# Two-layer backbone (window attention, latent attention): other homes and load points for norm weights, raw group weights, latent rows and rotary buffers; block sums of the first token half in three steps

## The chip, the core and the metric

The kernel runs on one core of one Trainium2 chip. A core has five engines that each work through their own instructions in order and meet at semaphores: TensorE (PE, matmuls and transposes; PEld its weight loads), VectorE (DVE), ScalarE (ACT), GpSimd (POOL) and SyncE (SP), which here mainly issues DMA transfers. The metric is the device time of one execution in microseconds, from runs on the chip; less is better.

## The reference

One batch of 1024 latent tokens and 256 context tokens, 1024 features, two layers. Layer 0 is grouped-query attention in a window (16 query heads, 4 key heads), layer 1 is multi-head latent attention; each layer is `x += gate * mixer(adaLN(rms_norm(x)))`. The change lies in the projections of layer 1:

```python
def project(h):                                   # h: 1024 latent + 256 context rows
    cq, ckv, kr, g = jnp.split(h @ w_in, [512, 768, 800], axis=-1)
    q = (rms_norm(cq, q_norm) @ w_uq).reshape(b, n, 16, 64 + 32)
    kv = (rms_norm(ckv, kv_norm) @ w_ukv).reshape(b, n, 16, 64 + 64)
    return q[..., :64], q[..., 64:], kv[..., :64], kr, kv[..., 64:], g

qrx = apply_rope(qrx, cos, sin); krx = apply_rope(krx, cos, sin)
s = (einsum("bqhd,bkhd->bhqk", qn, kn) + einsum("bqhd,bkd->bhqk", qr, kr)) * scale
y = (softmax(s) @ v * silu(g)) @ w_out
```

Everything is float32.

## The kernel before

**Arithmetic.** A float32 product is made of three PE products: each factor is split into a high part, rounded to the fast matmul format (a cast on ACT, L125), and the rest (a subtraction on DVE or POOL, L126); `mm3` then multiplies high by high, low by high and high by low (L130, L131, L132). So most operands pass ACT and then DVE or POOL before PE may use them.

**Memory.** On-chip memory is laid out by hand. Arena `F` has 52 slots of 1 KB per partition for float32 work, the arenas `R` and `K` hold split operands. A `Ring` is a list of places in an arena that are handed out in turn, over and over. Whatever is written into a place waits until its former content has been read; so the choice of places is also a choice of waits. Matmul results go to eight PSUM banks (`PB`).

**Order.** Up to the attention of layer 1 the order of instructions on each engine is set by a scheduler from the order in which the program is written, the dependences and its own estimates of durations; only the attention of layer 1 is ordered by hand. SP issues most DMAs, in order; small loads (`load2`) are issued by ACT.

**The stage that the change touches** is the projection of layer 1, L986 to L1400, from about 700 to 960 us of the span:

- `norm_x` (L229 to L234) loads 128 rows of x, takes the mean square (ACT L231), the power (POOL L233) and scales (DVE L234). `turn_h` transposes two such tiles on PE (L245), applies scale and shift on ACT into an x slot of 8 KB (L249; ring `xtr`), and splits (L253, L254).
- `kv_tile` multiplies one tile of 128 tokens with 288 columns of b_w_in, 24 products into one of three banks. The first 256 columns are the latent keys: normed with `rstd` (L1025 to L1027) and the weight `kvn` (DVE L1065); the other 32 are the rotary key (copied by ACT, L1066, which lets go of the bank). Then they are turned (L1071), split and written to `ckv_d` (L1075). The weight `kvn` is loaded on ACT's queue (L1042) into F 13, where the last output projection of layer 0 still adds its result (L706).
- `t_sums` builds, from two x slots, the sums of token blocks that the fast matrix product needs (Strassen-Winograd, seven products of half size in place of eight): T1 to T4, each split by a cast (L1100) and a subtraction (L1101). The sums L1095 to L1097 and L1104 are made in place, in the x slots.
- `Group` is one such product, 256 columns of b_w_in by all tokens. Groups 0 and 1 give the query latents (`cq`), groups 2 to 5 the gate. `fetch` loads raw weights (L1119) into the ring `wr`, `op` makes their sums on DVE (L1138 to L1152) in the ring `sr` and splits them (POOL makes the low part), `P(n)` does the products, adds earlier ones on DVE (L1172, L1178, L1186) into the ring `ov`, and `post` sends the result to DRAM: L1194 to `g_d` after a silu (L1193), L1200 to `cq_d`.
- `kr_rope` (L1085 to L1089) applies the rotary embedding to all keys, with two buffers of ring `er`, which shares F 8 to 10.5 with `sr`.
- `load_rows`, `scale_rows` bring the query latents back, norm and split them; `qr_tile` multiplies them with the rotary part of b_w_uq (block 3, `fetch1(3)`), `rope` (L281, L286, POOL L291) writes into the ring `ev` with temporaries from `rtmp`, and the result is turned (L1251) and written to `qr_d` from the ring `qst`. `qn_tile` does the other part. All weights of this part pass the staging ring `stg`.

Of the kernel before, what the change touches and what calls it, by code (L numbers as in the profile page):

```python
# [31 lines left out]
B_SCALE = 96 ** -0.5  # L32
# [28 lines left out]
def kernel(ctx: ExitStack, tc: tile.TileContext, t, out, dbg=None):  # L61
# [926 lines left out]
    sinb = f_at(1, 8, 32)  # L988
    kvn = f_at(13, 256)
    er = Ring(F, [8 + 1.25 * i for i in range(4)], 320)  # L990
# [4 lines left out]
    t4buf = f_at(4, 4, 256)  # L995
    p1s = [f_at(o, 512) for o in (22, 24, 49, 2, 49, 2)]
    ov = Ring(F, [34, 45, 47, 4, 6], 512)
    sr = Ring(F, [8, 10, 12], 512)
    sqacc = [f_at(37, 512), f_at(39, 512)]
    r_b = [f_at(41, 512), f_at(43, 512)]  # L1000
    cqr = Ring(F, [14, 16, 18, 20, 30, 32, 26, 28], 512)
    stg = Ring(F, [30, 32.25, 49.5], 576)
# [29 lines left out]
    for p in range(2):  # L1032
        xs = [norm_x(src1(2 * p + j), xr, junk) for j in range(2)]
        xts[p] = shp(xtr.next(), 8, 256)
        turn_h(p, xs, xts[p], hT1[p], ada1, range(4))
    load2(out=cosb, in_=t["cos_b"].rearrange("p (t d) -> p t d", t=8))
    load2(out=sinb, in_=t["sin_b"].rearrange("p (t d) -> p t d", t=8))
    for _ in last_outproj:
        pass
    load2(out=qncol, in_=t["q_norm_col"])  # L1040
    nc.vector.tensor_scalar_mul(qncol, qncol, B_SCALE)
    load2(out=kvn, in_=t["b_kv_norm"].partition_broadcast(128))  # L1042

# [38 lines left out]
    def kr_rope():  # L1082
        u = krF[:, 2:10, :]
        o, tmp = [shp(er.bufs[i], 8, 32) for i in range(2)]
        nc.vector.tensor_mul(o, u, cosb)  # L1085
# [5 lines left out]
    def t_sums(x0, x1, cs, t4):  # L1091
# [10 lines left out]

        put(T2, hb)
        sub(t4, lb, hb)  # L1104
        put(T1, la)
        put(T3, ha)
        return lambda: put(T4, t4)

# [99 lines left out]
    def latent_rms(step):  # L1208
# [15 lines left out]
        nc.gpsimd.tensor_tensor(rc, rc, mhalf.to_broadcast([128, 8]), ALU.pow)  # L1224

    def load_rows(h):
        rows = [cqr.next() for c in range(4)]
        for c, u in enumerate(rows):
            load(out=u, in_=cq_d[c, :, 512 * h : 512 * h + 512])
        return rows  # L1230
# [57 lines left out]
    def first_op(i, n):  # L1288
        groups[i].fetch((n - 1,), 1)
        groups[i].op(n)  # L1290

    t_rest = []
    order1 = [2 * p + j for p in (0, 1, 3, 2, 4) for j in range(2)]
    nx = norm_x(src1(order1[4]), xr, junk)
    for i, ti in enumerate(order1):
# [22 lines left out]
        if i == 3:  # L1318
            t_rest.append(t_sums(xts[1], xts[3], slice(0, 256), t4buf))
        if i in (5, 7):  # L1320
# [4 lines left out]
        if i > 7:  # L1325
            first_op(0, i - 7)
            first_op(1, i - 7)
        if i == 8:
            groups[0].P(1)
    groups[1].P(1)  # L1330
    flush()
    t_rest.append(t_sums(xts[2], xts[4], slice(256, 512), xts[2][:, 4:8]))
    wr = Ring(F, [30, 26], 1024)
    for f in t_rest:
        f()
    groups[0].fetch()
    groups[0].P(2)
# [3 lines left out]
    groups[1].fetch()  # L1341
    kr_rope()
    for gi, ns in todo:
        g = groups[gi]
        last = gi == 5
        ops = [] if last else list(todo[gi + 1][1])
        for i, n in enumerate(ns):
# [6 lines left out]
            if gi == 4 and i in (1, 3):  # L1354
                latent_rms(i)
            if gi == 4 and i == 5:
                rows = [load_rows(0)]
            if last and i == 0:
                rows.append(load_rows(1))
            if last and i == 2:  # L1360
                stg = Ring(F, [8, 10, 12, 22, 24], 512)
                fetch1(3)
            if last and i in (4, 5):
                scale_rows(i - 4, rows[i - 4])
    fetch1(4, nc.vector)
    ev = Ring(F, [34, 45, 47, 6], 512)
    rtmp = Ring(F, [49, 2], 512)
    qst = Ring(F, [14, 18, 30, 37, 41, 26], 1024)
    for ti in range(8):
# [550 lines left out]
```

## Time and profile before

| | |
|---|---|
| median of 3 runs | 1581.6 us (1580.81 to 1582.58) |
| the profiled execution | 1577.52 us, its span 1575.7 us |
| PE, DVE, ACT, POOL busy | 97%, 66%, 51%, 51% of the span |
| mean granted clock of PE | 0.988 |
| instructions | 25723, of them 9190 matmuls and transposes |

The span runs from the first to the last instruction of the profiled execution; its own time is 1.8 us longer. A row of the timeline reads: start and busy time in us, engine, line of the kernel, operation, what it writes, what it reads, shape, and in brackets how long the engine idled just before and what ended the idle time. A row of waits reads: engine, target and line, what ended the wait, then us in total, times, and the longest in us. A row of windows reads: the stretch in us, its length, busy time (and instructions) of PE, PEld, DVE, ACT and POOL, PE's granted clock as a share of full speed, the share of the DMA engines, GB/s. The names `arena_f`, `arena_r` and `arena_k` stand for any place in an arena.

### The profile page before, as it was taken

What the parts mean: (1) busy time and instruction counts of PE and PEld (TensorE: products, weight loads), DVE (VectorE), ACT (ScalarE), POOL (GpSimd) and SP (SyncE); (2) the same over time, 40 slices, a digit from 0 to 9 for tenths busy, and PEclk for the clock granted to TensorE, in tenths of its full rate; (3) what the DMA queues carried; (4) which work ended last, traced back from release to release, by engine and by line L of the source; (5) the groups of instructions that cost most, each with busy time, mean ns of one, the idle gap of its engine ahead of it and who ended that gap; (6) DMA issues with size and microseconds to landing.
All of it is one profiled execution on the core that took longest, in us unless ns stands there. A gap on an engine that the chain in (4) does not pass through costs nothing. (4 is left out here: it accounts for less than half of the span.)

```text
span 1575.7 us, 25723 instructions
## 1 busy us (share of the span) xinstructions
PE 1523.3 (97%) x9190; PEld 1187.6 (75%) x9190; DVE 1045.0 (66%) x1745; ACT 803.0 (51%) x1550; POOL 804.5 (51%) x840
## 2 busy tenths in 40 slices
PE   7999999999999999997989999999999999999998
PEld 4988888887878888877868778666766766766687
DVE  3878996657777777766654543677577677577354
ACT  4432322267777777767733523555555555555321
POOL 1151211136565444543375542688688688689410
PEclk9999999999999999998999999999999999999999
DMA  8357674653343333334354576223233232243251
GB/s 324 102 163 218 199 207 136 199 163 100 100 145 99 87 94 89 91 113 148 111 158 132 175 260 190 85 70 98 62 96 100 73 94 84 62 137 113 69 167 67
DMA packets 160078, 204.01 MB, mean 129 GB/s; under 512 B 14656, under 2 KB 94016, under 8 KB 159952
## 3 DMA queue, kind: packets, MB, share of 16 engines
q1 hardware_dynamic: 158480, 200.48, 42.5%
q10 hardware_dynamic: 1472, 1.90, 0.4%
q8 instruction: 72, 1.18, 0.3%
q14 instruction: 54, 0.44, 0.1%
HBM read 151.46 MB, written 50.87 MB: 128 GB/s over the span
## 5 line engine op out<-in xcount | busy, mean ns | idle before, releaser
L130 PE MATMUL PB<-arena_r 128*128 128x512 f32 (+2 forms) x990 | 368.8, 375 | 11.9 <-ACT arena_r L125 6.8
L1565 POOL TENSOR_TENSOR arena_f<-arena_f 128x512 f32<-128x512 f32 x252 | 328.4, 1303 | 82.0 <-ACT arena_f L1557 65.2
L131 PE MATMUL PB<-arena_r 128*128 128x512 f32 (+2 forms) x958 | 352.7, 369 | 1.3 <-POOL arena_r L685 0.8
L132 PE MATMUL PB<-arena_r 128*128 128x512 f32 (+2 forms) x926 | 339.7, 367 | 0.0
L126 POOL TENSOR_TENSOR arena_r<-arena_f,arena_r 128x512 fp32r<-128x512 f32 x106 | 148.1, 1409 | 280.9 <-ACT arena_r L125 231.0
L130 PEld LDWEIGHTS PB<-arena_r 128*128 128x128 f32 x990 | 187.5, 190 | 47.7 <-ACT arena_r L125 7.9
L1557 ACT ACTIVATE arena_f<-PB 128x1024 f32<-128x1024 f32 x160 | 164.1, 1026 | 109.4 <-PE PB L1551 69.1
L1516 DVE TENSOR_REDUCE arena_f<-PB 128x1 f32<-128x1024 f32 x128 | 156.0, 1218 | 86.4 <-PE PB L1514 86.3
L131 PEld LDWEIGHTS PB<-arena_r 128*128 128x128 f32 x958 | 182.4, 190 | 29.7 <-DVE arena_r L420 2.4
L132 PEld LDWEIGHTS PB<-arena_r 128*128 128x128 f32 x926 | 176.7, 191 | 29.0 <-issue 1.7
L1551 PE MATMUL PB<-arena_r 64*128 64x512 f32 (+1 forms) x1490 | 194.4, 392 | 0.3 <-ACT arena_f L1557 0.3
L1551 PEld LDWEIGHTS PB<-arena_r 64*128 64x128 f32 (+1 forms) x1490 | 135.8, 185 | 29.0 <-ACT arena_f L1557 1.8
L126 DVE TENSOR_TENSOR arena_r<-PB,arena_r 128x512 fp32r<-128x512 f32 (+1 forms) x171 | 115.7, 684 | 60.5 <-ACT arena_r L125 59.6
L1573 PE MATMUL PB<-arena_f 128*64 128x512 f32 x640 | 144.4, 597 | 0.0
L628 DVE CUSTOM_DVE_ANT_0 arena_f<-PB,arena_f,small 128x640 f32<-128x640 f32 (+2 forms) x176 | 125.1, 722 | 18.5 <-PE PB L617 11.8
L631 ACT ACTIVATE arena_f<-arena_f,small 128x640 f32<-128x640 f32 (+2 forms) x160 | 119.5, 747 | 34.8 <-DVE small L628 32.1
L125 ACT CAST arena_r<-arena_f 128x512 fp32r<-128x512 f32 (+1 forms) x139 | 83.5, 617 | 93.5 <-PE PB L132 26.4
L125 ACT CAST arena_r<-PB 128x512 fp32r<-128x512 f32 (+1 forms) x171 | 98.2, 582 | 46.0 <-PE PB L648 44.0
L617 PE MATMUL PB<-arena_k,arena_r 128*128 128x256 f32 (+1 forms) x576 | 111.6, 309 | 1.5 <-DVE small L628 1.3
L1573 PEld LDWEIGHTS PB<-arena_f 128*64 128x64 f32 x640 | 43.1, 136 | 83.2 <-issue 79.7
L648 PE MATMUL PB<-ident,arena_f 128*128 128x128 f32 x672 | 103.9, 274 | 0.8 <-DVE arena_r L126 0.3
L617 PEld LDWEIGHTS PB<-arena_k,arena_r 128*128 128x128 f32 x576 | 89.5, 188 | 14.1 <-DVE small L628 3.5
(246 smaller groups left out, 2634.2 us busy)
## 6 DMA issues: line engine op xcount, KB each, us to landing
arena_f<-ada_w SPq DMA_DIRECT2D x40, 512.0 KB, 4.7
arena_r<-q_d SPq DMA_DIRECT2D x80, 256.0 KB, 3.8
arena_r<-qn_d SPq DMA_DIRECT2D x64, 256.0 KB, 4.0
arena_r<-qr_d SPq DMA_DIRECT2D x170, 64.0 KB, 3.3
arena_f<-a_w_in SPq DMA_DIRECT2D x40, 256.0 KB, 3.5
g_d<-arena_f SPq DMA_DIRECT2D x32, 256.0 KB
q_d<-arena_f SPq DMA_DIRECT2D x64, 128.0 KB, 2.5
qn_d<-arena_f SPq DMA_DIRECT2D x16, 512.0 KB, 3.0
```

The source lines that it names most:

```text
L125: nc.scalar.copy(hi, src)
L126: (lo_eng or nc.vector).tensor_sub(lo, src, hi.bitcast(F32))
L130: nc.tensor.matmul(o, ah, bh, start=first, stop=False, skip_group_check=more)
L131: nc.tensor.matmul(o, al, bh, start=False, stop=False, skip_group_check=more)
L132: nc.tensor.matmul(o, ah, bl, start=False, stop=last, skip_group_check=more)
L617: nc.tensor.matmul(S[:, at : at + n], qT[:, s, hq, :], kT[:, g, k : k + n], start=s == 0, stop=s == 1)
L628: nc.vector.tensor_tensor_reduce(P[:, a:b], S[:, 256 + a : 256 + b], mk, 1.0, sk, ALU.add, ALU.min, to)
L1516: nc.vector.reduce_max(mx[:, 32 + b : 33 + b], flat, AX.X, negate=True)
L1551: nc.tensor.matmul(S[:, t], k[r, c : c + 128], q[r], start=j == 0, stop=j == 4)
L1557: nc.scalar.activation(E, self.S, AF.Exp)
L1565: eng.tensor_add(self.acc, self.acc, E[:, t])
L1573: nc.tensor.matmul(self.pv[p : p + 64], Vq[:, cs[t], self.h % 4, :], E[:, t], start=i == 0, stop=i == 4)
```

## The change

The change gives several buffers other places in arena F and moves some loads and a few computations in the written order. It adds no computation and takes none away.

- `kvn` lies in F 51 and is loaded ahead of the last output projection of layer 0, as is `qncol`.
- `t_sums` is a generator with three steps: the fourth sum and T1, then T2 and T3, then T4. For the first token half the first step follows the fourth kv tile, the second the sixth; for the second half both come at the end. T4 comes last for both.
- Group weights: the ring `wr` of the large pieces lies in F 22 and 26 in place of 30 and 26, and group 0's large pieces are fetched in the loop, at the last kv tile. First products (`p1s`), outputs (`ov`) and sums (`sr`, five places up to group 3, then three) have other places.
- `kr_rope` uses the place of `junk` (F 34.5) and runs ahead of the second products of groups 0 and 1.
- The first half of the latent rows is asked for in group 3, the second at the end of group 4, in F 22 and 24 in place of 30 and 32. The weights of the rotary part are loaded by the new `load_qr` in group 4, in a ring of three places, and split in group 5. That ring of three also stages all later weights, in place of five. `ev`, `rtmp` and `qst` have other places.

```diff
@@ -986,19 +986,19 @@
-    kvn = f_at(13, 256)
+    kvn = f_at(51, 256)
...
-    p1s = [f_at(o, 512) for o in (22, 24, 49, 2, 49, 2)]
-    ov = Ring(F, [34, 45, 47, 4, 6], 512)
-    sr = Ring(F, [8, 10, 12], 512)
+    p1s = [f_at(o, 512) for o in (45, 47, 49, 2, 45, 47)]
+    ov = Ring(F, [34, 30, 32, 4, 6], 512)
+    sr = Ring(F, [8, 10, 12, 41, 43], 512)
...
-    cqr = Ring(F, [14, 16, 18, 20, 30, 32, 26, 28], 512)
+    cqr = Ring(F, [14, 16, 18, 20, 22, 24, 26, 28], 512)
@@ -1033,13 +1033,13 @@
+    load2(out=qncol, in_=t["q_norm_col"])
+    nc.vector.tensor_scalar_mul(qncol, qncol, B_SCALE)
+    load2(out=kvn, in_=t["b_kv_norm"].partition_broadcast(128))
     load2(out=cosb, in_=t["cos_b"].rearrange("p (t d) -> p t d", t=8))
     load2(out=sinb, in_=t["sin_b"].rearrange("p (t d) -> p t d", t=8))
     for _ in last_outproj:
         pass
-    load2(out=qncol, in_=t["q_norm_col"])
-    nc.vector.tensor_scalar_mul(qncol, qncol, B_SCALE)
-    load2(out=kvn, in_=t["b_kv_norm"].partition_broadcast(128))
@@ -1081,7 +1081,7 @@
     def kr_rope():
         u = krF[:, 2:10, :]
-        o, tmp = [shp(er.bufs[i], 8, 32) for i in range(2)]
+        o, tmp = [f_at(34.5 + i, 8, 32) for i in range(2)]
@@ -1100,11 +1100,13 @@
-        put(T2, hb)
         sub(t4, lb, hb)
         put(T1, la)
+        yield
+        put(T2, hb)
         put(T3, ha)
-        return lambda: put(T4, t4)
+        yield
+        put(T4, t4)
@@ -1223,6 +1225,14 @@
+    def load_qr(ks):
+        sts = []
+        for k in ks:
+            st = stg.next()
+            load(out=st, in_=t["b_w_uq"][k * 128 : k * 128 + 128, 1024:1536])
+            sts.append(st)
+        return sts
@@ -1316,7 +1325,10 @@
         if i == 3:
-            t_rest.append(t_sums(xts[1], xts[3], slice(0, 256), t4buf))
+            t13 = t_sums(xts[1], xts[3], slice(0, 256), t4buf)
+            next(t13)
+        if i == 5:
+            next(t13)
@@ -1325,24 +1337,29 @@
+        if i == 9:
+            wr = Ring(F, [22, 26], 1024)
+            groups[0].fetch()
         if i == 8:
             groups[0].P(1)
     groups[1].P(1)
     flush()
-    t_rest.append(t_sums(xts[2], xts[4], slice(256, 512), xts[2][:, 4:8]))
-    wr = Ring(F, [30, 26], 1024)
-    for f in t_rest:
-        f()
-    groups[0].fetch()
+    t24 = t_sums(xts[2], xts[4], slice(256, 512), xts[2][:, 4:8])
+    next(t24)
+    next(t24)
+    kr_rope()
+    for f in (t13, t24):
+        next(f, None)
     groups[0].P(2)
     groups[1].P(2)
     for n in todo[0][1]:
         groups[0].op(n)
     groups[1].fetch()
-    kr_rope()
     for gi, ns in todo:
         g = groups[gi]
         last = gi == 5
+        if gi == 4:
+            sr = Ring(F, [8, 10, 12], 512)
@@ -1353,19 +1370,24 @@
-            if gi == 4 and i == 5:
+            if gi == 3 and i == 1:
                 rows = [load_rows(0)]
-            if last and i == 0:
+            if gi == 4 and i == 6:
                 rows.append(load_rows(1))
+                stg = Ring(F, [8, 10, 12], 512)
+                qrw = load_qr((0, 1, 2))
             if last and i == 2:
-                stg = Ring(F, [8, 10, 12, 22, 24], 512)
-                fetch1(3)
+                wt1[3] = r_at(wst1[3], 2, 4, 512)
+                for k in range(4):
+                    split(wt1[3][:, 0, k], wt1[3][:, 1, k], qrw[k], nc.gpsimd)
+                    if k == 0:
+                        qrw += load_qr((3,))
...
-    ev = Ring(F, [34, 45, 47, 6], 512)
-    rtmp = Ring(F, [49, 2], 512)
-    qst = Ring(F, [14, 18, 30, 37, 41, 26], 1024)
+    ev = Ring(F, [49, 2, 37, 39], 512)
+    rtmp = Ring(F, [41, 43], 512)
+    qst = Ring(F, [14, 18, 22, 26, 30, 45], 1024)
```

What the scheduler makes of it is shown at three places, as it stands in the engines' queues (line, operation, target, sources, shape; in the changed kernel the lines behind L1100 are two or more higher).

The first place is ACT around the third kv tile. The piece of the difference shows where the load of `kvn` stood.

```order
 L249 ACTIVATE arena_f<-PB,small 128x256
-L1042 DMA arena_f<-b_kv_norm 128x256
-L253 CAST arena_r<-arena_f 128x512
 L1025 ACTIVATE arena_f,small<-PB 128x256
-L125 CAST arena_r<-arena_f 128x512
+L253 CAST arena_r<-arena_f 128x512
 L1025 ACTIVATE arena_f,small<-PB 128x256
 L125 CAST arena_r<-arena_f 128x512
 L1066 COPY krF<-PB 128x32
 L231 ACTIVATE arena_f,small<-arena_f 128x1024
+L125 CAST arena_r<-arena_f 128x512
```

The load is gone from here; it now stands in the middle of layer 0's attention, some 240 rows earlier on ACT. The transposes of the next x tiles (L245) also stand elsewhere on PE: behind 7 products of the fourth kv tile, where there were 15.

The second place is DVE at the block sums of the first token half: L1104 (L1103 in the changed kernel) is the fourth sum, L1101 the low parts, of T2 in `arena_k`, of T1 and T3 in `arena_r`.

```order
 L234 TENSOR_SCALAR arena_f<-arena_f,small 128x1024
-L1104 TENSOR_TENSOR arena_f<-arena_f 128x1024
-L1101 TENSOR_TENSOR arena_k<-arena_f,arena_k 128x4x256
-L1101 TENSOR_TENSOR arena_r<-arena_f,arena_r 128x4x256 x2
+L1103 TENSOR_TENSOR arena_f<-arena_f 128x1024
+L1101 TENSOR_TENSOR arena_r<-arena_f,arena_r 128x4x256
 L1026 TENSOR_SCALAR small<-small 128x1
 L232 TENSOR_SCALAR small<-small 128x1
 L1026 TENSOR_SCALAR small<-small 128x1
+L1101 TENSOR_TENSOR arena_k<-arena_f,arena_k 128x4x256
 L1065 SCALAR_TENSOR_TENSOR arena_f<-PB,small,arena_f 128x256
```

T1's subtraction stands right behind the fourth sum, T2's behind three small operations, and T3's two scalings further on.

The third place is the start of the groups, first SP, whose queue holds the writes of the gate (L1194, then L1196) and the raw weights (L1119, then L1121).

```order
 L1075 DMA ckv_d<-arena_k 128x2x128 x2
-L1119 DMA arena_f<-b_w_in 128x4x128
-L1194 DMA g_d<-arena_f 128x512
+L1196 DMA g_d<-arena_f 128x512
+L1121 DMA arena_f<-b_w_in 128x4x256
 L1075 DMA ckv_d<-arena_k 128x2x128 x4
-L1119 DMA arena_f<-b_w_in 128x4x128
-L1194 DMA g_d<-arena_f 128x512
-L1119 DMA arena_f<-b_w_in 128x4x256
-L1075 DMA ckv_d<-arena_k 128x2x128 x2
+L1121 DMA arena_f<-b_w_in 128x4x128
+L1196 DMA g_d<-arena_f 128x512
```

In the changed kernel the second write of the gate, group 3's, comes from F 30, and the next raw piece of 128 columns (`128x4x128`, not in the piece) goes into F 30. And DVE at the same place, before:

```order
L1144 TENSOR_TENSOR arena_f<-arena_f 128x512
L1152 TENSOR_TENSOR arena_f<-arena_f 128x512
L1085 TENSOR_TENSOR arena_f<-krF,arena_f 128x256
L1088 TENSOR_TENSOR arena_f<-krF,arena_f 128x16x8 x2
L1144 TENSOR_TENSOR arena_f<-arena_f 128x512
L1172 TENSOR_TENSOR arena_f<-PB,arena_f 128x512
```

and in the changed kernel:

```order
L1101 TENSOR_TENSOR arena_k<-arena_f,arena_k 128x4x256
L1085 TENSOR_TENSOR arena_f<-krF,arena_f 128x256
L1088 TENSOR_TENSOR arena_f<-krF,arena_f 128x16x8 x2
L1140 TENSOR_TENSOR arena_f<-arena_f 128x512
L126 TENSOR_TENSOR arena_r<-PB,arena_r 128x256
```

The key rope (L1085, L1088) stands ahead of group 0's sums, where it stood behind them and ahead of group 1's.

More of the change, by code (lines that the diff above doesn't have):

```diff
@@ L1290, in first_op @@
         groups[i].op(n)
-    t_rest = []
     order1 = [2 * p + j for p in (0, 1, 3, 2, 4) for j in range(2)]
```

## The prediction

> **What bounds the kernel now.** The first view is the page's table of engines, with the windows of time beside it.
>
> ```profile
> PE 1523.3 (97%) x9190; PEld 1187.6 (75%) x9190; DVE 1045.0 (66%) x1745; ACT 803.0 (51%) x1550; POOL 804.5 (51%) x840
> ...
> 700.00:930.00 230.00, 207.46 (x1027) 174.41 (x1026) 131.61 (x202) 119.23 (x239) 111.80 (x95) 0.94 0.51 156
> ...
> 1000.00:1040.00 40.00, 40.00 (x294) 25.97 (x296) 25.21 (x31) 20.19 (x23) 33.60 (x27) 1.00 0.27 70
> ```
>
> TensorE (PE) is busy 97% of the span. The change removes no matmul, so only PE's idle time and its clock are to be had, and only in the stage that it touches: from 700 to 930 us PE idles 22.5 us at a mean granted clock of 0.94. Behind it, at 1000 us, PE is busy without a gap, so what is saved ahead comes through to the end.
>
> The second view, PE's waits, names the stalls; the third, narrow windows behind the long ones, shows what they cost twice.
>
> ```profile
> PE PB L130 <- ACT arena_r L125: 7.5, 3, 6.1
> PE PB L130 <- DVE arena_f L1178: 2.0, 2, 1.3
> ...
> 726.90:733.70 6.80, 6.07 (x26) 6.05 (x27) 3.27 (x9) 4.56 (x12) 3.40 (x5) 0.50 0.16 43
> 747.30:754.10 6.80, 6.14 (x20) 4.96 (x21) 5.45 (x12) 5.92 (x16) 1.89 (x3) 0.50 0.43 139
> 802.00:808.80 6.80, 3.23 (x8) 2.59 (x9) 3.63 (x4) 1.96 (x4) 5.19 (x4) 0.50 0.54 142
> 911.10:917.90 6.80, 5.45 (x15) 4.49 (x16) 3.16 (x7) 1.10 (x2) 5.03 (x4) 0.50 0.61 181
> 894.00:896.00 2.00, 1.01 (x4) 0.86 (x5) 2.00 (x4) 2.00 (x5) 0.00 (x0) 1.00 0.75 254
> ```
>
> Four stalls of over 3 us (rows below) each bring 6.8 us at clock 0.50. Half of PE's busy time there is lost: 3.0, 3.1, 1.6 and 2.7 us. The stall of 1.28 us at 894 us kept the clock at 1.00.
>
> **Part 1, the latent norm weight kvn gets a home and a load of its own.**
>
> ```profile
> 718.77 0.87 SPq L229 DMA_DIRECT2D arena_f<-x_d  x2
> 719.72 0.33 ACTq L1042 DMA_DIRECT2D arena_f<-b_kv_norm  x1
> 726.88 0.48 DVE L1065 SCALAR_TENSOR_TENSOR arena_f<-PB,small,arena_f 128x256 f32<-128x256 f32 x1 [4.33 <-DMA arena_f<-b_kv_norm]
> 727.39 0.18 ACT L1066 COPY krF<-PB 128x32 f32<-128x32 f32 x1 [2.78 <-DVE arena_f L1065]
> 727.48 1.06 ACT L231 ACTIVATE arena_f<-arena_f 128x1024 bf16<-128x1024 f32 x1
> 727.63 0.61 PE L130 MATMUL PB<-arena_k,arena_r 128*128 128x288 f32 x1 [3.25 <-ACT krF L1066]
> 729.84 0.75 DVE L234 TENSOR_SCALAR arena_f<-arena_f,small 128x1024 f32<-128x1024 f32 x1 [1.02 <-POOL small L233]
> ...
> DMA to landing us min/median/max: 3.5/4.5/7.4
> ```
>
> The load is issued at 719.72, DVE waits 4.33 us for it, ACT then copies and frees the PSUM bank, and PE resumes after 3.25 us. Now the load stands in the middle of layer 0's attention, so this wait goes: 3.25 + 3.0 = 6.3 us. (It stays on ACT's own DMA queue; its 0.33 us of issue lies in the attention, and ACT is busy 51% of the span.) Late next are the rows of x (two loads from 718.77; the last row is how long such loads take). PE's order now has the turn (L245) that needs them behind 7 products of the fourth kv tile instead of 15, so PE would get there at 724.4 + 7 x 0.133 = 725.3. From a landing at 718.8 + 4.5 to 7.4 = 723.3 to 726.2, the square on ACT, the power on POOL and the scale on DVE follow; from L231's start to L234's end they take 727.48 to 730.59, 3.1 us. So the turn could start at 726.4 to 729.3. A new stall of 1.1 to 4.0 us; I take 3.1, two thirds of the way, as x's loads share the queue with a raw weight piece. What waits behind L245 on PE is the rest of the fourth tile, 8 products, and nothing else is at hand for PE. It would be split at 726.9, where the clock changed in the old run (the changes lie 20.4, 54.7 and 109.1 us apart, 6, 16 and 32 times 3.41): 1.6 us idle ahead of it and 1.5 behind, less than half of either stretch of 3.41, and I take it that the clock stays. **Gain 6.3 - 3.1 = 3.2**, bounds 0 (the longest stall, and the clock lost again) and 5.2.
>
> **Part 2, block sums in three steps.**
>
> ```profile
> 743.45 0.66 PE L245 MATMUL PB<-ident,arena_f 128*128 128x128 f32 x4 [0.99 <-DVE arena_f L234]
> 745.58 2.35 DVE L1101 TENSOR_TENSOR arena_r<-arena_f,arena_r 128x1024 fp32r<-128x1024 f32 x2
> 746.89 1.47 ACT L249 ACTIVATE arena_f<-PB,small 128x256 f32<-128x256 f32 x3 [1.83 <-DVE arena_r L1101]
> 747.96 1.12 PE L245 MATMUL PB<-ident,arena_f 128*128 128x128 f32 x4 [3.86 <-ACT arena_f L249]
> ...
> 743.94:747.35 3.41, 0.16 (x2) 0.00 (x0) 3.41 (x4) 1.55 (x5) 0.00 (x0) 0.99 0.00 0
> ```
>
> PE waits 3.86 us for L249, which writes the x slot that T2's, T1's and T3's subtractions still read on DVE. In the new order T1 follows the fourth sum at once and T2 and T3 stand later. What L249 waits for is then T1, which comes one subtraction (2.35 / 2 = 1.2 us) earlier than the end of the pair it was in. The 0.99 us ahead is the chain from the x load and stays. So the stall falls to 2.7 us; it would still lie inside one 3.4 us window that is then about 21% busy (0.16 + 1.2 - 0.66 = 0.7 of 3.41; 0.66 is how far the stall now reaches past 747.3), and the one ahead of 726.9, idle from 727.63 - 3.25 = 724.4 on and so 27% busy, was followed by half clock. **Gain 1.2**, bounds 0 and 3.86 + 3.1 = 7.0.
>
> The Trainium skill, TensorE: Matmul & The Clock Gate, "Why this matters for your kernels", allows PE gaps up to about 3 us. By it the stall of 2.7 us keeps the clock, and the sum would be 3.1 us better. The trace speaks against that: half clock began at 726.9, 2.5 us into the idle time.
>
> **Part 3, group weights, outputs and sums.** One wait is new. Output buffers are now 34, 30, 32, 4, 6, so group 3's gate goes to 30, where the next raw piece of group 0 lands; the SP order shows the write to g_d ahead of that load.
>
> ```profile
> 773.91 0.29 PE L130 MATMUL PB<-arena_k,arena_r 128*128 128x288 f32 x1
> 774.71 0.30 PE L130 MATMUL PB<-arena_k,arena_r 128*128 128x288 f32 x1
> 781.73 1.30 POOL L126 TENSOR_TENSOR arena_r<-arena_f,arena_r 128x512 fp32r<-128x512 f32 x1 [1.82 <-ACT arena_r L125]
> 850.00:860.00 10.00, 10.00 (x46) 8.28 (x45) 3.53 (x6) 4.35 (x7) 3.89 (x3) 1.00 0.46 132
> cq_d<-arena_f SPq DMA_DIRECT2D x8, 256.0 KB, 3.6
> arena_f<-b_w_in SPq DMA_DIRECT2D x8, 256.0 KB, 2.8
> ```
>
> From the end of group 3's second product: silu 0.6 (as the cast at 890.98, 4.26 / 8), issue 0.3, write (the nearest is cq_d, 3.6), load 2.8, cast 0.6 and POOL's low half 1.3: 9.2 us. PE has 39 products of 288 columns (0.133 each, six between the two PE rows), four transposes (some 0.4) and five of 512 (10/46 = 0.22): 6.7 us, and 0.4 more before the low half is needed. 9.2 - 7.1 = 2.1; with the issue hidden, **stall 2.0**. Behind the cast ACT's queue holds a kv tile's square and bank copy, which PE reaches later than the products that it waits for; on SP the second piece stands behind the first, and the writes of ckv_d behind both, for which nobody waits before 900 us. Bounds of the loss 0 and 7 (a write of 8.6 us is seen at 901 us, below).
>
> ```profile
> 795.62 0.43 DVE L1085 TENSOR_TENSOR arena_f<-krF,arena_f 128x256 f32<-128x256 f32 x1 [3.89 <-POOL arena_r L126]
> 797.29 1.76 DVE L1144 TENSOR_TENSOR arena_f<-arena_f 128x512 f32<-128x512 f32 x1 [0.85 <-POOL krF L1089]
> 803.08 1.74 DVE L1152 TENSOR_TENSOR arena_f<-arena_f 128x512 f32<-128x512 f32 x1 [1.16 <-POOL arena_r L126]
> 804.74 0.68 DVE L1178 TENSOR_TENSOR arena_f<-PB,arena_f 128x512 f32<-128x512 f32 x1
> 805.57 0.77 PE L130 MATMUL PB<-arena_r 128*128 128x512 f32 x1 [6.09 <-ACT arena_r L125]
> ```
>
> The stall of 6.09 us is labelled as ACT's, but that cast is the following group's. PE resumes right behind L1178, which frees its bank (804.74 + 0.68). L1178 stands on DVE behind three waits: the key rope for POOL, since its buffers are sum slots (3.89), then 0.85 and 1.16, together 5.9. With the rope elsewhere and ahead of the second products, and five sum slots, all three go (the rope's own 0.43, 0.48 and 0.73 us stay, under PE's products of that time), and PE would find 0.2 us left. With the clock (1.6) that is 7.5; bounds 4 (a raw piece late) and 7.7. The small stalls (7.5 - 6.1 and 2.0 - 1.3, and 0.4 at L1071: 2.5) come from the ring of three; five slots remove POOL's wait, yet the sums then stand at the raw loads: **0.9** of them, bounds 0 and 2.5. **Gain 8.4** together.
>
> **Part 4, the latent rows, rotary weights and buffers.**
>
> ```profile
> 890.98 4.26 ACT L125 CAST arena_r<-arena_f 128x512 fp32r<-128x512 f32 x8 [1.12 <-DMA arena_f<-b_w_uq]
> 894.99 0.50 PE L130 MATMUL PB<-arena_k,arena_r 128*128 128x512 f32 x1 [1.28 <-DVE arena_f L1178]
> 901.03 0.34 SPq L1194 DMA_DIRECT2D g_d<-arena_f  x1
> 909.70 0.69 DVE L281 TENSOR_TENSOR arena_f<-PB,arena_f 128x512 f32<-128x512 f32 x1 [4.82 <-DMA g_d<-arena_f]
> 911.13 1.26 POOL L291 TENSOR_TENSOR arena_f<-arena_f 128x512 f32<-128x512 f32 x1 [3.96 <-DVE arena_f L286]
> 912.45 1.11 PE L1251 MATMUL PB<-ident,arena_f 128*128 128x128 f32 x4 [3.52 <-POOL arena_f L291]
> ```
>
> The rotary weights (b_w_uq) are loaded a group earlier, so ACT's casts of the latent rows no longer queue behind such a load: **gain 1.3**, bounds 0.5 and 1.3. SP issues these four loads ahead of g_d's last writes, 0.4 us each, with no one waiting. A rotary tile wrote into the buffer that g_d's last write, issued at 901.03, still read until 909.7. The new rope buffers are not output buffers: 3.52 + 2.7 = **6.2**. POOL's first L291 now stands behind two low halves, 2.6 us, which the 4.82 that DVE waits no longer covers; bounds 3 and 6.2. The staging ring has three buffers instead of five for the 20 pieces that follow. A round of load 3.7, cast 0.6 and low half 1.3 is 5.6 us, 1.9 a piece. **Loss 0.5**, bounds 0 and 4.
>
> **The sum.** 3.2 (part 1) + 1.2 (part 2) - 2.0 + 8.4 (part 3) + 1.3 + 6.2 - 0.5 (part 4) = 17.8 us. The profiled execution took 1577.5 us (its span 1575.7): 1559.7. The runs' median is 1581.6, 4.1 more, which belongs to the executions and not to the stage: **1564**. The eight terms' distances to their bounds, added as squares, are 7 us to the better side and 8 to the worse: 1557 to 1572.
>
> **The rivals.**
> - **All stalls go, the clock's losses too** (1555): the x rows land at 723.3 (stall 1.1), the second stage keeps its clock, nothing waits at buffer 30. Sum 5.2 + (1.2 + 3.1) + 0 + (7.7 + 2.5) + 1.3 + 6.2 = 27. For it: every stall has one named cause that the change removes. Against: the x load is not earlier. Chance 0.18. The page TensorE: Matmul & The Clock Gate of the Trainium skill, with its 3 us, is on this side.
> - **The first half gives nothing** (1571): the x rows cost what kvn did and the write to g_d takes 3 us more than cq_d's; 0 + 1.2 - 5 + 8.4 + 7.0 - 0.5 = 11. For it: both are chains through DRAM. Chance 0.20.
> - **The change doesn't do what it says** (1581): DVE and POOL serve the group stage at the old pace, because the raw loads set it, and the order alone has moved. Against: the three waits of 5.9 us name POOL, not a DMA. Chance 0.05.
> - **Slower** (1585): the staging ring. 20 pieces through three buffers take 6.7 us for each us of a round. The qr and qn tiles and what follows cover about 70 us (890 to 960), so it decides from a round of 10.5 us; if loads take 11.5 us beside the latent transfers, a round is 13.4, 90 us in all, 20 late, more than the 17.8 gained. Against: pieces land in 3.7 today in the same stretch. Chance 0.05.
>
> **How the numbers follow.** Forecast 0.52 (1557 to 1572), rivals 0.18, 0.20, 0.05, 0.05. A measurement of this kernel can tell about 0.2%, 3.2 us, from no change. Faster by more: 0.90; within: 0.05; slower: 0.05. Range 1554 to 1575, which leaves out the last two and part of the second.
>
> **What would show it.** Right: no wait for b_kv_norm at L1065; an L245 stall of 2 to 4 us near 728; the second stall at 2.7; a wait of PE of about 2 us behind the raw load after group 3's first products; no gap above 1 us around 800 and at the first rotary tile; granted clock 1.00 there. Wrong: half clock after the L245 stall, a raw load as the releaser of DVE in each group, ACT waiting for b_w_uq or b_w_ukv with PE behind it from 890 us on.

## The result and the profile after

| | changed kernel | before, same chip | ratio, 95% interval |
|---|---|---|---|
| median (fastest to slowest), us | 1573.1 (1572.4 to 1573.9) | 1581.2 (1579.6 to 1582.6) | 0.9949 [0.9932, 0.9966] |
| the same kernel a second time (`e11_after_again`) | 1573.1 | 1578.5 | 0.9966 [0.9954, 0.9978] |
| profiled execution, us (span) | 1573.9 (1572.2) | 1577.5 (1575.7) | |

The change makes the kernel faster, by 5 to 8 us where 17.6 were forecast (1564 from 1581.6). The spans of the two profiles differ by only 3.5 us, since the executions reach the stage at different times: between 691.1 and 698.0 us over the fourteen profiles of this document, and those of before and its variants (692.7 to 696.5) lie inside that range. So from here on the stage itself is measured: from the issue of the first x load of layer 1 to the first score product of layer 1. By form of instruction, the groups of before give both ends (the times behind the durations are the first and the last start):

```profile
L229 SPq DMA_DIRECT2D arena_f<-x_d x10: 332/379/491, 693.4 to 750.2; - x10
L1514 PE MATMUL PB<-arena_r x512: 385/393/501, 970.1 to 1451.4; 64*128 64x512 f32 x171
```

and those of the changed kernel:

```profile
L229 SPq DMA_DIRECT2D arena_f<-x_d x10: 319/399/767, 696.8 to 751.9; - x10
L1536 PE MATMUL PB<-arena_r x512: 385/393/501, 966.7 to 1448.1; 64*128 64x512 f32 x171
```

The stage took 970.1 - 693.4 = 276.7 us and takes 966.7 - 696.8 = **269.9, 6.8 less**. Behind it both kernels run alike (481.3 and 481.4 us between the last two times of the score rows).

The table of engines and the windows of the changed kernel (sum of the window, PE, PEld, DVE, ACT, POOL, mean clock, DMA share and GB/s) stand against those of before:

```profile
PE 1523.9 (97%) x9190; PEld 1184.9 (75%) x9190; DVE 1042.1 (66%) x1745; ACT 802.7 (51%) x1550; POOL 806.2 (51%) x840
...
700.00:930.00 230.00, 211.87 (x1063) 177.36 (x1063) 132.41 (x212) 122.65 (x248) 116.47 (x97) 0.97 0.53 162
733.70:737.10 3.40, 3.40 (x17) 3.38 (x17) 2.74 (x5) 2.28 (x7) 0.55 (x1) 0.54 0.23 68
750.75:754.15 3.40, 3.40 (x14) 2.79 (x13) 3.40 (x6) 2.93 (x6) 0.40 (x1) 0.54 0.36 96
784.60:788.00 3.40, 3.40 (x8) 2.75 (x9) 2.94 (x5) 0.68 (x3) 1.67 (x2) 0.50 0.61 154
822.40:825.80 3.40, 3.14 (x8) 2.57 (x9) 0.81 (x2) 0.63 (x1) 3.20 (x3) 0.53 0.15 18
```

No engine's busy time moved by more than 3 us. The clock is up from 0.94 to 0.97 between 700 and 930 us, but there are still four stretches at half clock: 3.4 us long now, not 6.8, so each costs half of PE's busy time in it, 1.5 to 1.7. The waits of PE in the changed kernel (total, count, longest) name what is late:

```profile
PE PB L245 <- DVE small L1026: 4.4, 1, 4.4
PE PB L130 <- ACT arena_r L125: 3.9, 4, 1.8
PE PB L130 <- DVE arena_f L1180: 3.3, 1, 3.3
PE PB L245 <- ACT arena_f L249: 3.1, 2, 2.7
PE PB L1261 <- POOL arena_r L126: 1.9, 2, 1.2
```

No label names a DMA, but the timeline below shows one behind several. Term by term (measured: stalls and lost clock of before, 6.3, 7.9, none, 9.6 and 7.5 us, less those that stand now; the sum of the 9.6 is 6.1 + 0.4 + 0.7 + 0.8 + 1.6 of clock):

| term | forecast | measured | what stands there now |
|---|---|---|---|
| 1, kvn | +3.2 | +0.2 | 6.3 became 4.4 + 1.7 of clock |
| 2, block sums | +1.2 | +2.7 | stalls 2.7 + 0.5 + 0.3, clock 1.7 in place of 3.1 |
| 3, the wait at F 30 | -2.0 | -4.6 | stalls 1.8 + 1.1, clock 1.7 |
| 3, rope and sum slots | +8.4 | +3.2 | stalls 3.3 + 0.9 + 0.7, clock 1.5 |
| 4, latent rows, rotary | +7.0 | +5.6 | stalls 1.2 + 0.8 |
| sum | +17.8 | +7.1 | the stage: +6.8 |

The timeline of the changed kernel at the five terms (start, duration, engine, line; in brackets the idle time ahead and what ended it):

```profile
721.80 1.31 SPq L229 DMA_DIRECT2D arena_f<-x_d  x2
729.00 1.06 ACT L231 ACTIVATE arena_f<-arena_f 128x1024 bf16<-128x1024 f32 x1 [2.95 <-DMA arena_f<-x_d]
731.00 1.75 DVE L234 TENSOR_SCALAR arena_f<-arena_f,small 128x1024 f32<-128x1024 f32 x1 [0.66 <-POOL small L233]
732.80 0.66 PE L245 MATMUL PB<-ident,arena_f 128*128 128x128 f32 x4 [4.44 <-DVE small L1026]
...
749.25 0.66 PE L245 MATMUL PB<-ident,arena_f 128*128 128x128 f32 x4 [2.72 <-ACT arena_f L249]
...
775.73 0.33 SPq L1196 DMA_DIRECT2D g_d<-arena_f  x1
777.77 0.37 SPq L1121 DMA_DIRECT2D arena_f<-b_w_in  x1
781.00 0.18 ACT L1066 COPY krF<-PB 128x32 f32<-128x32 f32 x1 [4.01 <-DVE arena_f L1065]
781.09 1.05 ACT L1100 CAST arena_k<-arena_f 128x1024 fp32r<-128x1024 f32 x1
782.03 0.62 ACT L125 CAST arena_r<-arena_f 128x512 fp32r<-128x512 f32 x1
782.71 0.50 PE L130 MATMUL PB<-arena_r 128*128 128x512 f32 x1 [1.77 <-ACT arena_r L125]
784.57 0.78 PE L131 MATMUL PB<-arena_r 128*128 128x512 f32 x1 [1.14 <-POOL arena_r L126]
...
800.64 8.09 POOL L126 TENSOR_TENSOR arena_r<-arena_f,arena_r 128x512 fp32r<-128x512 f32 x5
808.76 0.38 SPq L1121 DMA_DIRECT2D arena_f<-b_w_in  x1
813.00 0.69 DVE L1140 TENSOR_TENSOR arena_f<-arena_f 128x512 f32<-128x512 f32 x1 [4.83 <-DMA arena_f<-b_w_in]
...
822.66 0.77 PE L130 MATMUL PB<-arena_r 128*128 128x512 f32 x1 [3.26 <-DVE arena_f L1180]
...
925.34 0.62 ACT L125 CAST arena_r<-arena_f 128x512 fp32r<-128x512 f32 x1 [2.44 <-DMA arena_f<-b_w_ukv]
927.32 0.63 PE L1261 MATMUL PB<-ident,arena_f 128*128 128x128 f32 x4 [1.16 <-POOL arena_r L126]
```

First, ACT's square of x waited for the rows, 7.2 us from issue at 721.8, and PE's 4.44 us are that chain, whatever releaser the label names. Third, at F 30, the load was issued 2.0 us behind the write (775.73 to 777.77) and landed 2.8 us later by the view of that issue, at 780.6. The cast started some 1.4 us after that, at 782.03: ACT works in order, and ahead of the cast stood the bank copy L1066, which waited 4.01 us for DVE's L1065, and a cast of 1.05 us. PE waited for the cast and then for POOL's low half. Fourth, the key rope no longer stands there, yet PE waits 3.26 us one group later: POOL runs five low halves back to back to 808.73, the next raw load is issued only then, at 808.76, DVE waits 4.83 us for it and then 1.84 us for POOL itself (ahead of L1146, at 819.04), and L1180, which frees the bank, comes late. Last, a piece of b_w_ukv lands late, ACT casts late, and the rotary tile stands on POOL behind the low half.

### The profile page after: what moved, and what is told of

Its sections match the earlier page's. It is cut to its first block, busy times and chain, and to the rows that moved or that the text cites. A ratio compares the mean times of both kernels' runs of the same rounds, so it can differ in the third digit from the quotient of the medians.

```text
span 1572.2 us, 25724 instructions
## 1 busy us (share of the span) xinstructions
PE 1523.9 (97%) x9190; PEld 1184.9 (75%) x9190; DVE 1042.1 (66%) x1745; ACT 802.7 (51%) x1550; POOL 806.2 (51%) x840
## 5 line engine op out<-in xcount | busy, mean ns | idle before, releaser
L125 ACT CAST arena_r<-arena_f 128x512 fp32r<-128x512 f32 (+1 forms) x139 | 83.6, 617 | 103.3 <-PE PB L132 17.8
```

The source lines that it names most:

```text
L125: nc.scalar.copy(hi, src)
```

## The experiments

The theory was that four chains take the place of the four that went: the x rows in part 1, the write to g_d at F 30, POOL's low halves in the group stage, and the staging ring of three in part 4. The rival for the group stage was the raw loads. Ratios are to the kernel before; stages compare with 269.9 (changed) and 276.7 (before).

A stage is that of one profiled execution, and parts of it move that an edit doesn't touch: the stall of part 1 at L245 ran from 2.79 to 4.44 us over the nine profiles that have kvn's new home and POOL's first low halves, and half clock came and went with it. So an edit is also read in its own place. For the group stage that is the stalls and the lost clock behind 785 us: 9.6 us before (with the 0.4 at L1071), 6.4 in the changed kernel.

**`e1_kvn_back`**: kvn at its old home and load point, all else changed.

```diff
-    kvn = f_at(51, 256)
+    kvn = f_at(13, 256)
...
-    load2(out=kvn, in_=t["b_kv_norm"].partition_broadcast(128))
...
     for _ in last_outproj:
         pass
+    load2(out=kvn, in_=t["b_kv_norm"].partition_broadcast(128))
```

> The changed kernel with kvn alone back at F 13, loaded behind the last output projection. Measure: the stage from the issue of the first layer-1 x load to the first score product (276.7 us before, 269.9 after). Theory (the rows of x took over from kvn, and the clock fell again): the part is worth nothing; the PE stall of 3.2 us at the bank copy comes back, the 4.4 us stall at L245 goes, the stage stays at 270 within 1 us. Rival (kvn is worth the 3.2 us predicted, and the loss is elsewhere): stage at 273, the 4.4 us stall at L245 stays in part beside the new one.

Measured: 1572.1 us, 0.9964 [0.9951, 0.9978], stage 271.5. In its timeline the old stall is back in place of the new one:

```profile
731.77 0.40 PE L130 MATMUL PB<-arena_k,arena_r 128*128 128x288 f32 x1 [3.62 <-ACT krF L1066]
```

The 1.6 us more of stage lie elsewhere: in its own place the old stall cost 3.62 and 1.7 of clock, 5.3, where the new one cost 6.1. So part 1 is worth nothing that the runs can tell: one wait was exchanged for another.

**`e5_no_x_load`**: the changed kernel without the load of the sixth x tile, every other instruction in its place.

```diff
-    def norm_x(src, xr, junk):
+    def norm_x(src, xr, junk, ld=True):
         x = xr.next()
-        load(out=x, in_=src)
+        ld and load(out=x, in_=src)
...
-                nx = norm_x(src1(order1[n + 1]), xr, junk)
+                nx = norm_x(src1(order1[n + 1]), xr, junk, n != 4)
```

> The changed kernel without the load of one tile of x rows (the sixth tile of layer 1, into F 45); the tile is then worked out from the rows that lay there, so this computes other numbers. All else keeps its place and order. Theory (the 4.4 us stall of PE at L245 is the landing of this load, which is what the kvn load had covered): the stall falls under 1.5 us, the half clock behind it goes, stage (first layer-1 x load to first score product; 269.9 in the changed kernel) 264 to 266. Rival (the stall is the chain through ACT, POOL and DVE that stands behind the kv tiles' own norms, as its label, a DVE scalar of the latent norm, says): the stall stays over 3 us, stage 269 to 271.

Measured: 1570.2 us, 0.9942 [0.9920, 0.9964], stage 267.4. The timeline and two windows of this kernel:

```profile
725.78 1.75 DVE L234 TENSOR_SCALAR arena_f<-arena_f,small 128x1024 f32<-128x1024 f32 x1 [0.67 <-POOL small L233]
727.58 0.66 PE L245 MATMUL PB<-ident,arena_f 128*128 128x128 f32 x4 [2.79 <-DVE small L1026]
```

```profile
722.99:726.39 3.40, 1.79 (x14) 1.56 (x12) 1.16 (x3) 2.44 (x7) 2.74 (x4) 1.00 0.06 23
726.39:729.80 3.41, 2.22 (x18) 2.22 (x19) 2.08 (x5) 2.19 (x6) 1.69 (x3) 1.00 0.27 77
```

Without any load PE still waits 2.79 us: power and scale queue behind other work on POOL and DVE. The load is 1.65 of the 4.44 in this pair of executions. And a stall of 2.79 us that straddles two stretches, PE 53% and 65% busy, kept the clock. Theory and rival were each half right.

**`e7_sums_back`**: the block sums in their old order.

```diff
+        put(T2, hb)
         sub(t4, lb, hb)
         put(T1, la)
-        yield
-        put(T2, hb)
         put(T3, ha)
+        yield
         yield
```

> The changed kernel with the block sums in the old order (T2, fourth sum, T1, T3 at once). Theory (T1's subtraction is what the reuse of the x slot waits for, and the shorter stall also halves the time at half clock): the stall at L249 grows from 2.7 to 3.9 us and the half clock from one 3.4 us stretch to two, stage 272 to 273. Rival (the order of the sums is worth nothing): stage 269.5 to 270.5.

Measured: 1572.8 us, 0.9959 [0.9944, 0.9974], stage 271.2, 1.3 more. The stall at L245 grows from 2.72 to the old 3.86, as part 2 has it, but behind it stays one stretch of 3.4 us at half clock where the theory had two:

```profile
749.32 0.66 PE L245 MATMUL PB<-ident,arena_f 128*128 128x128 f32 x4 [3.86 <-ACT arena_f L249]
```

**`e2_gate_f47`**: group 3's gate goes out from F 47, so no load follows a write in F 30.

```diff
-    ov = Ring(F, [34, 30, 32, 4, 6], 512)
+    ov = Ring(F, [34, 47, 32, 4, 6], 512)
...
         if i == 8:
+            ov.bufs[1] = f_at(30, 512)
             groups[0].P(1)
```

> The changed kernel with group 3's gate output in F 47 instead of F 30, so that no raw piece of group 0 waits for the write to DRAM. Theory (the write and the load behind it are the stall at 782 us): the stalls of 1.77 and 1.14 us and the half clock behind them (1.7 us) go, 4.6 us; up to half of it may be given back in the groups, where raw weights are late: stage 265 to 268. Rival (ACT and POOL would be late there anyway): a stall of over 1.5 us stays at these products, stage 269 to 270.

Measured: 1567.2 us, 0.9934 [0.9912, 0.9957], stage 265.5, 4.4 less. The stalls of 1.77 and 1.14 us are gone and the half clock with them; the group stage now has 2.76 and smaller ones in place of the 3.26:

```profile
789.80 0.50 PE L131 MATMUL PB<-arena_k,arena_r 128*128 128x512 f32 x1 [2.76 <-POOL arena_r L126]
```

Of the 4.4 us, 1.5 lie at the L245 stall of part 1, which was 3.13 us here. What stood at F 30, 4.6 us with its clock, is gone, and the places behind it now hold 7.6 us of stalls (1.27 at L1071, 2.76, 1.58, 1.15 and 0.87) where they held 6.4. The new home also let the scheduler reorder ACT and PE: the cast now stands ahead of ACT's cast L1100. So the run shows that the wait goes with this home, but not that the load is what PE waited for: the rival, that ACT would be late there anyway, stays open.

**`e3_raw_four`**: four places for the large raw pieces, so that the loads no longer stand behind POOL.

```diff
-            wr = Ring(F, [22, 26], 1024)
+            wr = Ring(F, [22, 26, 14, 18], 1024)
...
+                    if not ops and gi == 3:
+                        wr = Ring(F, [22, 26], 1024)
...
-            if gi == 3 and i == 1:
+            if gi == 4 and i == 1:
                 rows = [load_rows(0)]
```

> The changed kernel with four places for raw group weights (F 22, 26, 14, 18) in place of two, up to group 4; the first half of the latent rows is asked for in group 4. Theory (a group's raw weights can be loaded only when POOL has made the low half of the last one's, so each group runs through load, DVE, ACT and POOL one after the other): DVE's waits for b_w_in (25.8 us in the changed kernel) fall under 10, the 3.3 us stall at 822 us and its half clock go, stage 264 to 266. Rival (POOL's own work is the bound in the groups): DVE waits for POOL in place of the load, a stall of over 2 us stays, stage 269 to 270.

Measured: 1572.0 us, 0.9956 [0.9942, 0.9969], stage 274.9, 5.0 more, in an execution that was the slowest of ten; the median is 1.1 us under the changed kernel's. DVE's waits for raw weights, 25.8 us in eight waits in the changed kernel, fell to these (total, count):

```profile
DVE arena_f L1140: 5.0, 2
DVE arena_f L1146: 3.7, 1
```

and its timeline has the stall all the same:

```profile
790.63 0.68 DVE L1142 TENSOR_TENSOR arena_f<-arena_f 128x512 f32<-128x512 f32 x1
795.36 5.97 POOL L126 TENSOR_TENSOR arena_r<-arena_f,arena_r 128x512 fp32r<-128x512 f32 x4
796.69 1.76 DVE L1142 TENSOR_TENSOR arena_f<-arena_f 128x512 f32<-128x512 f32 x1 [4.66 <-POOL arena_r L126]
811.31 0.76 PE L130 MATMUL PB<-arena_r 128*128 128x512 f32 x1 [4.36 <-DVE arena_f L1180]
```

The loads come early and DVE then waits for POOL. The loads as the cause fall: POOL sets the pace, and most of the waits for late loads followed from it.

**`e6_low_dve`**: the low halves of the groups' sums on DVE in place of POOL; PE's and SP's order does not change.

```diff
-        def put(self, src):
+        def put(self, src, eng=None):
             s = shp(wslot.next(), 2, 4, 128)
-            split(s[:, 0], s[:, 1], src, nc.gpsimd)
+            split(s[:, 0], s[:, 1], src, eng)
...
-                self.A11 = self.put(raw(0, 0))
+                self.A11 = self.put(raw(0, 0), nc.gpsimd)
...
-                self.A12 = self.put(raw(0, 1))
+                self.A12 = self.put(raw(0, 1), nc.gpsimd)
```

> The changed kernel with the low halves of the groups' sums and of the fourth raw block made on DVE in place of POOL; PE and SP keep their order. Theory (after four raw places did not help: POOL's low halves, 1.3 us each, are what paces the first groups, and they hold the raw places and the sum places as well): the stall of 3.3 us at 822 us goes with its half clock, those of 0.9 and 0.7 us too, stage 264 to 266. Rival (the raw loads pace the groups: 4 us of load behind the last reader of a place): a stall of over 2 us stays, stage 269 to 271. Second rival: DVE, now with 3.5 us more work in each group, holds up PE elsewhere: a new stall ended by DVE, stage 270 or more.

Measured: 1566.2 us, 0.9923 [0.9903, 0.9943], stage 262.5, 7.4 less. Groups by line from 785 to 870 us (count, busy total, mean ns, idle ahead) in the changed kernel:

```profile
L1154 DVE TENSOR_TENSOR arena_f<-arena_f 128x512 f32<-128x512 f32 x5 | 7.1, 1418 | 0.1
L126 POOL TENSOR_TENSOR arena_r<-arena_f,arena_r 128x512 fp32r<-128x512 f32 x32 | 44.8, 1416 | 27.6 <-ACT arena_r L125 27.5
```

and in `e6_low_dve`, then its timeline at the stall's place:

```profile
L126 DVE TENSOR_TENSOR arena_r<-arena_f,arena_r 128x512 fp32r<-128x512 f32 x30 | 21.0, 708 | 4.0 <-ACT arena_r L125 4.0
L1154 DVE TENSOR_TENSOR arena_f<-arena_f 128x512 f32<-128x512 f32 x6 | 5.2, 866 | 0.0
```

```profile
802.36 0.47 PE L130 MATMUL PB<-arena_r 128*128 128x512 f32 x1 [0.83 <-DVE arena_f L1180]
```

A low half takes 0.71 us on DVE and 1.42 on POOL, and DVE's sums at L1154 take 0.87 in place of 1.42, with five low halves left on POOL in that time. The 3.26 us stall is gone, and the group stage lost 0.8 us where it lost 6.4; that is 5.5 of the 7.4 us. The rest lies at L245, where the stall was 2.79 us and kept the clock. The run does not part the two effects, POOL's slower low half and DVE's slower sums beside it.

**`e10_rope_sums_only`** and **`e12_before_low_dve`** make one edit each to the kernel before: the rope and the five sum slots of part 3 alone, and the low halves on DVE alone (the diff of `e6_low_dve`).

```diff
-    sr = Ring(F, [8, 10, 12], 512)
+    sr = Ring(F, [8, 10, 12, 41, 43], 512)
...
-        o, tmp = [shp(er.bufs[i], 8, 32) for i in range(2)]
+        o, tmp = [f_at(34.5 + i, 8, 32) for i in range(2)]
...
     for f in t_rest:
         f()
+    kr_rope()
     groups[0].fetch()
...
     groups[1].fetch()
-    kr_rope()
...
+        if gi == 4:
+            sr = Ring(F, [8, 10, 12], 512)
```

> The kernel before with one part of the change alone: the key rope in the place of junk and ahead of the second products, and five sum places up to group 3. Theory (POOL paces the first groups, so the wait removed at the rope comes back one or two groups on): the 6.1 us stall goes, one or more stalls of 2 to 4 us in all appear in the next groups, stage 271.5 to 274 (276.7 before). Rival (the part is worth the 8.4 us predicted, and the changed kernel lost it by another part): stage 268 to 269.5.

> The kernel before with one edit: the low halves of the groups' sums and of the fourth raw block on DVE in place of POOL; PE keeps its order. Theory (POOL is the cause of the 6.1 us stall at 805 us, through the sum places that the rope and the sums wait for): that stall falls under 1.5 us and the 0.7 us ones go, stage 267 to 270 (276.7 before). Rival (shared places hold up the rope whichever engine makes the low halves): the stall stays over 3 us, stage 273 or more.

Measured: `e10_rope_sums_only` 1576.2 us, 0.9988 [0.9978, 0.9999], stage 274.7, 2.0 less than before; `e12_before_low_dve` 1569.0 us, 0.9944 [0.9926, 0.9962], stage 267.9, 8.8 less. In the first the wait for kvn, which its edit doesn't touch, was shorter and kept the clock (3.25 us and 3.0 of clock before); the largest stall left in place of the 6.09 us is the second row:

```profile
725.67 0.40 PE L130 MATMUL PB<-arena_k,arena_r 128*128 128x288 f32 x1 [1.71 <-ACT krF L1066]
792.68 0.79 PE L131 MATMUL PB<-arena_k,arena_r 128*128 128x512 f32 x1 [2.52 <-POOL arena_r L126]
```

in the second there is this:

```profile
801.47 0.47 PE L130 MATMUL PB<-arena_r 128*128 128x512 f32 x1 [0.82 <-DVE arena_f L1178]
```

The term for which 8.4 us were forecast brings 2.0 of stage by itself, and in its own place less: with stalls of 0.30, 0.73, 2.52, 1.44, 1.56 and 0.95 us and 1.5 of clock the group stage still loses 9.0 of the 9.6. Moving the low halves, with the rope left between the sums, removes the same stall and brings 8.8, where the whole change brought 6.8; the group stage loses 2.3 of the 9.6 (the 95% intervals of the two kernels' ratios overlap a little). DVE's wait of 3.89 us ahead of the rope came from POOL's pace, and other slots alone do not cure it.

**`e4_stage_six`**: six staging places from b_w_ukv on.

```diff
         if i == 3:
+            stg = Ring(F, [8, 10, 12, 34, 4, 6], 512)
             for k in range(2):
```

> The changed kernel with six staging places for the b_w_ukv pieces (F 8, 10, 12, 34, 4, 6) in place of three. Theory (the two stalls of 1.16 and 0.78 us at 927 and 931 us come from ACT waiting for a staged piece, with POOL's rope behind it): both go, stage 268. Rival (POOL's low halves stand ahead of the rope whatever the staging): stalls of 1.5 us or more stay, stage 270.

Measured: 1572.0 us, 0.9956 [0.9940, 0.9973], stage 270.5. The second rotary stall (0.78) is gone, the first stays with another releaser:

```profile
923.08 0.63 PE L1261 MATMUL PB<-ident,arena_f 128*128 128x128 f32 x4 [1.19 <-DVE arena_f L126]
```

The stage gained nothing, as half clock lasted 6.8 us behind the L245 stall in this execution. The staging ring is not shown to be what holds the first rotary tile.

**`e8_three_edits`** puts the edits of `e2_gate_f47`, `e6_low_dve` and `e4_stage_six` together; **`e9_all_low_dve`** moves, on top of these three, the low halves of the groups' first blocks as well; **`e11_after_again`** is the changed kernel beside them.

```diff
-            split(s[:, 0], s[:, 1], src, nc.gpsimd)
+            split(s[:, 0], s[:, 1], src)
```

> The changed kernel with three edits together: group 3's gate in F 47, low halves of the groups' sums on DVE, six staging places for b_w_ukv. If each keeps its own gain (4.4 measured, 4 to 6 expected, 1 expected): stage 258 to 261. If the groups give back what the earlier start saves: 263 to 266.

> The three edits together (group 3's gate in F 47, six staging places, groups' low halves on DVE), and the low halves of the first blocks on DVE too. Theory (the floor of 2.8 us of the L245 stall is POOL: its low halves of 1.6 us stand ahead of the power of the latent norm and draw out DVE's scaling of x from 0.75 to 1.75 us): the stall at L245 falls to 1.5 to 3.5 us, by when the rows land, stage 257 to 260. Rival (these low halves on DVE now stand ahead of the scaling themselves): the stall stays at 2.8 to 4.4 us, stage 261 to 263.

> The changed kernel once more, as a measure of how its stage differs between executions: 269.9 the first time, 270.5 in a kernel that differs from it behind this stage only. All theories: 269 to 271, the L245 stall between 2.8 and 4.5 us by the landing of the rows.

Measured: `e8_three_edits` 1563.1 us, 0.9896 [0.9881, 0.9911], stage 261.1; `e9_all_low_dve` **1557.7 us, 0.9878 [0.9859, 0.9896]**, stage 255.6; `e11_after_again` 0.9966 [0.9954, 0.9978], stage 269.9. The kernel of `e9_all_low_dve` is faster than the kernel before and the changed one; its interval overlaps that of `e8_three_edits`. In its timeline even the L245 stall of part 1 is short. No low half stands on POOL ahead of the powers there, and DVE's L234 takes 0.75 us in place of 1.75:

```profile
727.37 0.66 PE L245 MATMUL PB<-ident,arena_f 128*128 128x128 f32 x4 [1.20 <-DVE arena_f L234]
```

In `e11_after_again` that stall was 3.11 us, a stall of 2.17 stood elsewhere, and half clock came in three stretches, not four. So single stalls of one kernel move by 1.3 to 1.4 us between executions, while the stage came out the same; the group stage lost 6.9 us there and 6.4 the first time.

## Why the prediction fell short

The bound was read rightly: PE's work did not change, what came off ahead of 930 us came through to the end, and each old stall went where the forecast said it would. The new stalls were undersized. Of the 10.7 us between 17.8 and 7.1 about half lie in one term (5.2, the rope and sum slots); part 1 lacks 3.0, F 30 2.6 and part 4 1.4, and part 2 gave 1.5 more. The rival "the first half gives nothing" (1571) came nearest in time and had part 1 and F 30 right in size (0 and -5), but it too counted on the 8.4.

1. **The step that failed: "all three go ... and PE would find 0.2 us left"** (part 3, forecast 8.4, measured 3.2). It took the waits of 3.89, 0.85 and 1.16 us as due to sum slots. They name POOL, and POOL was late because its low halves take 1.4 us each and come in bursts; more slots only move the point where DVE, or the raw load behind POOL, waits. `e10_rope_sums_only` (0.6 of the 9.6 in its place), `e3_raw_four` (the loads freed, the stall stays) and `e6_low_dve` and `e12_before_low_dve` (POOL freed, the stall goes) show it. The slow sums stood in the rows that were quoted, 1.74 us for a sum of two SBUF operands beside 0.68 for one with a PSUM operand, and were not asked about. The 2.5 us of small stalls were 1.9: the third wait in the row of 7.5 us, 0.7, stands behind 960 us. The rival that "DVE and POOL serve the group stage at the old pace" was near; its reason, the raw loads, was wrong.
2. **Part 1 (3.2, measured 0.2)** had the right successor, the x rows, inside its bounds (0 to 5.2). The chain behind the landing was 3.8 us, not 3.1, as L234 took 1.75 and not 0.75, the load took 7.2, and the clock, which "stays", fell.
3. **The F 30 wait (-2.0, measured -4.6)** had the right place, but its first stall, 1.8 us, came near the forecast by luck. Write and load took 2.0 and 2.8 us where 3.6 and 2.8 were taken, so by the term's own sum about 0.5 us would have been left; the rest was ACT's queue, which the term put aside. What it left out is a second stall at the low half (1.1) and half clock (1.7).
4. **Part 2 (1.2, measured 2.7)**: the stall came out at 2.72 against 2.7. The rest is half clock of 3.4 us where 6.8 were taken, and a smaller stall ahead; `e7_sums_back` gives the order 1.1 us of stall and none of the clock.
5. **Part 4 (7.0, measured 5.6)**: the write to g_d no longer holds the rotary buffer. The loss of 1.9 in new stalls was put at 0.5; what sets the first of them stays open after `e4_stage_six`.

## What to carry to other kernels

When a stall names an engine, ask why that engine is late before giving it more buffers: here POOL's pace moved every wait on to the next buffer, and moving its work to DVE, though DVE is the busier engine, was worth at least as much as all the new homes. Give each removed stall a successor with its own chain worked out, the queues of the engines on it included, and each new stall its price in clock. Test the suspected term alone on the old kernel, and read it in its own place; there it was worth 0.6 of 8.4.

## What the runs showed of the hardware

- A sum of two SBUF operands on DVE took 0.68 us with POOL idle and 1.76 us beside POOL's low halves (`e3_raw_four`, the L1142 rows). A sum with a PSUM operand took 0.68 beside them (the kernel before, L1178 at 804.74, with POOL's low halves from 799.78 to 807.19). The Trainium skill, SBUF — State Buffer, "SBUF: two separate sides", describes a port pair that DVE and GpSimd share under an exclusive lock; the rows agree with it.
- In this stage half clock followed from how busy PE was in a fixed stretch of 3.4 us, not from the length of one gap. These windows of the changed kernel stand just ahead of its four stretches at half clock:

```profile
730.30:733.70 3.40, 0.90 (x7) 0.90 (x8) 2.08 (x4) 2.38 (x7) 2.33 (x3) 0.96 0.07 9
747.35:750.75 3.40, 1.19 (x6) 0.88 (x7) 2.93 (x7) 2.67 (x9) 2.52 (x3) 0.96 0.00 0
781.20:784.60 3.40, 0.76 (x3) 0.33 (x3) 1.99 (x4) 3.40 (x7) 1.87 (x2) 1.00 0.10 29
819.00:822.40 3.40, 0.40 (x2) 0.00 (x0) 2.92 (x3) 0.00 (x0) 3.40 (x4) 0.97 0.23 77
```

PE is busy 12% to 35% in them, and 53% and 65% in those of `e5_no_x_load`, which kept the clock. Two stalls of 1.77 and 1.14 us with little between them lost it; one of 2.79 across two stretches did not. On this grid of stretches, from 690 to 970 us of all fourteen profiles, every stretch at full clock with PE busy up to 43% was followed by half clock, and from 46% on a single one was (50%, `e7_sums_back` at 780.7). Half clock ended after 3.4 us where PE was busy for about 84% or more of the slow stretch, and went on where it was less. The busy share is not the whole rule: outside the stage seven stretches with 53% to 92% were followed by half clock too (92% in `e3_raw_four` at 237.7 us), and why stays open.
